# A hybrid attention block on one core: the low part of the queries on 128 rows, queries loaded by halves

## The chip, the cores and the metric

The kernel runs on one core of a Trainium2 chip. A core has the engines TensorE (PE), VectorE (DVE), ScalarE (ACT) and GpSimd (POOL); SyncE (SP) issues the DMAs here, in the order in which they stand on its queue. The metric is the device time of one execution in microseconds, as the median of several runs.

## The reference

One layer over 1024 tokens of width 1024 in float32. After an RMSNorm a combined projection feeds two groups of heads. Group A, which matters here, is sparse attention: an indexer scores all keys for each query, the 256 best are kept, and each of 8 heads (width 64) attends to these.

```
score = sum over index heads of relu(q_idx . k_idx) * w        # masked by chunk
sel   = top 256 keys of each query                             # shared by all heads
logits = q . k / sqrt(64) + bias[bucket(key - query)]          # masked
o_a    = softmax(logits) @ v
```

Group B is gated linear attention. Then come the output projection with a residual, RMSNorm, a SwiGLU feed-forward of width 2816 with a residual, and a last RMSNorm.

## The kernel before

**Two parts for each number.** Matmul operands are float32 values rounded to the matmul's format (fp32r) and a low part that holds the rest. A product then takes three matmuls: high x high, high x low, low x high. In the attention the keys of a head, `Ks[h]`, have both parts in one tile of 128 rows: 64 rows hold the high part and the other 64 the low part (for odd heads the other way round). The high query part, 64 rows, is loaded twice, into both halves of the rows of a tile `q1`, so that one matmul with 128 rows gives high x high plus high x low.

**The low query part** is in a tile `ql`: 128 rows, with two heads one above the other and 4 such head pairs side by side. Its matmul takes only the 64 rows of its head (`r`) and only the high rows of the keys:

```
mm(lg[:, c0:c1], QL[p][r, h // 2, o], Ks[h][r, c0:c1], start=False, stop=True,
```

**One score tile** is made by `softmax(p, h, e)` (L1315): head h and 128 queries, tile t = 2p + e, against the n = 128(t+1) keys up to it. The keys are cut into chunks of up to 512 columns, so tiles 0 to 3 have one chunk and tiles 4 to 7 two. On PE, in this order: for each chunk the high query part times the keys (L1327) and, for the last 256 columns, two matmuls with an identity `eye` that add the position bias `nb` (L1331); then for each chunk the low query part (L1334). DVE adds the mask and takes the row minimum (L1340, for pair 0 L1342), ACT takes the exponential (L1346), DVE a reciprocal (L1348), and POOL scales (L1350). `value` (L1353) transposes the result on PE (L1363), splits it into two parts on ACT (L1375) and DVE (L1378), and multiplies it with the values `Vs` (L1387). `combine` joins the two halves of the output and stores them (`d_ma`, L1419).

**Order.** The program is written by a planner: each piece of work is a generator ("thread") with a rank. It asks for events, for slots of a pool or for time on an engine, and the planner, with its own costs, picks which thread issues its instructions next. The order on every engine and on SP's queue is fixed by this; on the chip semaphores make an instruction wait for its data. Pairs of query tiles come in the order 1, 2, 3, 0. `softmaxes` (L1425) starts score tiles when there are slots (`ahead`: 6 tiles of probabilities, `pl`: 2 wide score banks), and `values` follows. For head 5 of a pair it sets the event "load next", which lets `load_attention` (L1270) load the next pair: the queries (L1296, L1300), then values not yet there (L1307), then the event "load". The event of the last pair lets `main` start `load_out` (rank 1, three pages for each output tile) and the splitting of the output weights (rank 5: ACT L257, POOL L262); `load_attention` has rank 15.

**Pages.** Most tiles of SBUF are pages of one pool of 41. In the attention they hold 8 tiles of keys, up to 8 of values, 4 of bias, up to 5 of masks, 6 of probabilities, 4 of split transposes and 3 of queries for each pair (two `q1`, one `ql`). `finish_pair` gives a pair's pages back when its last output is made.

Of the kernel before, what the change touches and what calls it, by code (L numbers as in the profile page):

```python
# [10 lines left out]
F32R = mybir.dt.float32r  # L11
# [8 lines left out]
P = 128  # L20
# [27 lines left out]
def f32(ap):  # L48
    return ap.bitcast(F32)


PE, ACT, DVE, POOL, DMA = range(5)


def act(n, acc=False):
    return n / 1.2 + (280 if acc else 50)


def dve(n):
    return n / 0.96 + 68  # L60


def pool1(n):
    return n * 0.836 + 160
# [6 lines left out]
def pe(n, passes=1):  # L71
    return n * passes / 2.38
# [249 lines left out]
def block_kernel(ctx: ExitStack, tc: tile.TileContext, a: dict, out: bass.AP, dbg=None):  # L322
    nc = tc.nc
# [16 lines left out]
    def page(shape, dt, name):  # L340
        return big.tile(shape, dt, name=name, tag="pg", bufs=NPG)

    def bank(name="bank"):
        return pp.tile([P, HB], F32, name=name, tag="ps", bufs=4)

    def wide(name="wide"):
        return pp.tile([P, 2 * HB], F32, name=name, tag="pl", bufs=2)

    def small(shape, dt, name, bufs=2):
        return sm.tile(shape, dt, name=name, bufs=bufs)  # L350
# [4 lines left out]
    def quarter(shape, dt, name):  # L355
        return sm.tile(shape, dt, name=name, tag="kb", bufs=NKB)
# [8 lines left out]
    mm = nc.tensor.matmul  # L365
# [97 lines left out]
    fl = Flow()  # L463
    ev = fl.event
    pg = Slots(fl, NPG - NT - 1)
# [4 lines left out]
    LOAD = 2500  # L470
# [376 lines left out]
    d_q = [dr.tile([2, 512, HB], F32, name=f"d_q{i}") for i in range(2)]  # L847
# [398 lines left out]
    Ks, Vs, Q1, QL, nb = {}, {}, {}, {}, []  # L1246
# [23 lines left out]
    def load_attention():  # L1270

        for j in range(NT):
            yield ev("va", j)
        for hf in range(2):
            for c in range(4):
                yield ev("qa", hf, c)
        have = 0
        for at, p in enumerate(PAIRS):
            if at == 0:
                for i in range(4):  # L1280
                    yield ev("nb", i)
                    yield pg
                    yield DMA, 450
                    nb.append(page([P, 2, 2, 256], F32R, "nb"))
                    nc.sync.dma_start(f32(nb[i]), d_nb[i])
            else:
                yield ev("load next", at)
            q = []
            hf, o = p // 2, (p % 2) * 256
            for i in range(2):  # L1290
                yield pg
                yield DMA, 900
                q.append(page([P, 4, 256], F32R, "q1"))
                for s in range(2):
                    src = d_q[hf][0, i * 256:(i + 1) * 256, o:o + 256].rearrange("(h p) n -> p h n", p=64)
                    nc.sync.dma_start(f32(q[i][s * 64:(s + 1) * 64, :, :]), src)  # L1296
            yield pg
            yield DMA, 450
            l = page([P, 4, 256], F32R, "ql")
            nc.sync.dma_start(f32(l), d_q[hf][1, :, o:o + 256].rearrange("(c p) n -> p c n", p=P))  # L1300
            Q1[p], QL[p] = q, l
            ev("Q", p).set(LOAD)
            for j in range(have, 2 * p + 2):
                yield pg
                yield DMA, 450
                Vs[j] = page([P, AH, P], F32R, "V")
                nc.sync.dma_start(f32(Vs[j]), d_va[j])  # L1307
            have = max(have, 2 * p + 2)
            ev("load", p).set(LOAD)

    PB, OP = {}, {}
    units = [(p, h) for p in PAIRS for h in range(AH)]
# [2 lines left out]
    def softmax(p, h, e):  # L1315
        t = 2 * p + e
        n = (t + 1) * P
        o = slice(e * P, (e + 1) * P)
        r = slice((h % 2) * 64, (h % 2) * 64 + 64)
        yield PE, 2 * pe(n) + 2 * pe(256) if t else 380  # L1320
        if t == 4:
            lg, chunks = wide("lg")[:, P:P + n], ((0, 384), (384, 640))
        else:
            lg, chunks = wide("lg") if p else bank("lg"), [(c, min(n, c + HB)) for c in range(0, n, HB)]
        for c0, c1 in chunks:
            d0 = max(c0, n - 256)
            mm(lg[:, c0:c1], Q1[p][h // 4][:, h % 4, o], Ks[h][:, c0:c1], start=True, stop=False,  # L1327
               skip_group_check=True)
            for s in range(2):
                if d0 < c1:  # L1330
                    mm(lg[:, d0:c1], eye, nb[h // 2][:, s, h % 2, 256 - n + d0:256 - n + c1],  # L1331
                       start=False, stop=False, skip_group_check=True)
        for c0, c1 in chunks:
            mm(lg[:, c0:c1], QL[p][r, h // 2, o], Ks[h][r, c0:c1], start=False, stop=True,  # L1334
               skip_group_check=True)
        pb = PB[t, h] = page([P, n], F32, "pb") if p else quarter([P, 256], F32, "pb")[:, :n]
        mn = small([P, 1], F32, "mn", 6)
        yield DVE, dve(n)
        if p:
            nc.vector.tensor_tensor_reduce(pb, lg[:, :n], acc[t][:, :n], 1.0, 3e38, ALU.add, ALU.min, mn)  # L1340
        else:
            nc.vector.tensor_scalar(pb, lg[:, :n], 0.0, 3e38, op0=ALU.add, op1=ALU.min, accum_out=mn)  # L1342
        (pl if p else ps).give()
        yield ACT, act(n, True)
        se = small([P, 1], F32, "sume", 6)
        nc.scalar.activation(pb, pb, AF.Exp, bias=mn, scale=-1.0, accum_out=se)  # L1346
        yield DVE, 75
        nc.vector.reciprocal(se, se)  # L1348
        yield POOL, pool1(n) + 80
        nc.gpsimd.tensor_scalar(pb, pb, se, 1.0, op0=ALU.mult, op1=ALU.mult)  # L1350
        ev("p", t, h).set()
# [73 lines left out]
    def softmaxes():  # L1425
        for _ in range(NAHEAD + NPAIRS):
            yield pg
        at = 0
        for n, (p, h) in enumerate(units):
            if h == 0:  # L1430
                at += 1
                yield ev("load", p)
                if p == 0:
                    ev("softmax").set()
                    fl.spawn(give_back(ahead, NAHEAD), 0)
            for hf in range(p // 2 + 1):
                yield ev("ka", hf, h // 2)
            for e in range(2):
                if p:
                    yield ev("mask", 2 * p + e)  # L1440
                    yield ahead
                    yield pl
                else:
                    yield kb
                    yield ps
                if h == 5 and e == 0:
                    ev("load next", at).set()
                fl.spawn(softmax(p, h, e), 16.5 + n)

    def give_back(slots, n):  # L1450
        for _ in range(n):
            yield slots
            pg.give()

    def values():
        for n, (p, h) in enumerate(units):
            for e in range(2):
                yield ev("p", 2 * p + e, h)
            if h % 2 == 0:
                yield ps  # L1460
                OP[p, h // 2] = bank("av")
            for i in range(p + 1):
                if p:
                    yield pairs
                else:
                    yield hp
                    yield hp
                yield ps
                fl.spawn(value(n, i), 18.2 + n - 0.1 * i)
            if h % 2:  # L1470
                fl.spawn(combine(n), 16 + n)
            if h == 7:
                fl.spawn(finish_pair(p, n), 19 + n)
            if n == 8 * 3 - 1:
                fl.spawn(give_back(pairs, NPAIRS), 0)

    def finish_pair(p, n):
        yield ev("av", n, p)
        pg.give(n=[3 + 8 + 2 + 4, 3 + 1, 3 + 2, 3 + 2 + 6][p])
        ev("pair", p).set()  # L1480


# [717 lines left out]
    def main():  # L2200
# [19 lines left out]
        yield from proj_f(evac_qa, 1)  # L2220
        yield from proj_f(evac_ka, 0)
        fl.spawn(load_attention(), 15)
        fl.spawn(softmaxes(), 16)
        fl.spawn(values(), 17.5)
        yield from proj_f(evac_ka, 1, True)
# [61 lines left out]
```

## Time and profile before

| | us |
|---|---|
| median of 3 runs | 1335.14 (1332.27 to 1335.7) |
| the profiled execution | 1333.15 |
| its span, first to last instruction | 1331.3 |
| PE, DVE, ACT, POOL busy in the span | 1268.2, 968.9, 621.1, 444.1 |

The attention scores run from 417 to 578 us of the span; the first 417 us hold the projections, the indexer with its selection and the linear attention, and from 600 us on come the feed-forward products. Times of rows are microseconds from the span's start. [...]

### The profile page before, as it was taken

The numbers are of one execution on the slowest core, as the hardware profiler recorded it, in microseconds if no ns is written. First come the engines' busy times: TensorE is split into PE (matmuls) and PEld (weight loads), VectorE is DVE, ScalarE is ACT, GpSimd is POOL, SyncE is SP. The second block draws the span as 40 slices with busy tenths as digits, with TensorE's granted clock in tenths as the row PEclk, the third lists the DMA queues.
The fourth block names the chain that finished last, engine by engine and source line by source line (L and its number), as shares of the span: only waits on it lengthen the run. The fifth ranks groups of instructions, "written<-read, shape, count | busy, mean of one in ns | idle before, by whom it ended". The sixth has DMA issues, their size and how long they took to land.

```text
span 1331.3 us, 18081 instructions
## 1 busy us (share of the span) xinstructions
PE 1268.2 (95%) x6074; PEld 1028.8 (77%) x6074; DVE 968.9 (73%) x1900; ACT 621.1 (47%) x1139; POOL 444.1 (33%) x410
## 2 busy tenths in 40 slices
PE   5999999969999999989987999999999999999997
PEld 5878868746787888868865888888888888888886
DVE  5379998989996788724387788889776664435885
ACT  4467678554544677632143444444444432222232
POOL 4324324533311444561244343435333220000351
PEclk8999989979998999989988999999999999999999
DMA  7654221234471233565212676777667549555664
GB/s 217 182 145 127 67 60 49 95 127 167 170 233 46 74 112 112 164 209 206 87 40 80 221 263 235 269 263 266 221 222 237 182 170 381 200 197 190 206 252 174
DMA packets 122812, 230.22 MB, mean 173 GB/s; under 512 B 14120, under 2 KB 70240, under 8 KB 122720
## 3 DMA queue, kind: packets, MB, share of 16 engines
q1 hardware_dynamic: 122720, 229.07, 51.3%
q8 instruction: 48, 0.79, 0.3%
q14 instruction: 44, 0.36, 0.1%
HBM read 146.19 MB, written 82.85 MB: 172 GB/s over the span
## 4 chain that ended last, share of the span: by engine, by line
PE 75%; DVE 16%; issue 3%; DMA 2%; ACT 2%; POOL 1%; SPq 1%; POOLq 0%; DVEq 0%; ACTq 0%
DVE junk_v L756 6%; PE av L1387 3%; PE fc L1769 3%; PE fa L1769 3%; PE fa L1770 3%; PE fc L1770 3%; PE fa L1771 3%; PE fc L1771 3%; PE fb L1771 3%; PE fb L1770 3%; PE da L2085 3%; PE da L2083 3%; PE da L2084 3%; PE fb L1769 3%; PE ptr L1363 3%
## 5 line engine op out<-in xcount | busy, mean ns | idle before, releaser
L1594 POOL TENSOR_TENSOR w<-raw,w 128x512 fp32r<-128x512 f32 x66 | 96.8, 1469 | 181.9 <-ACT w L1730 140.7
L262 POOL TENSOR_TENSOR w<-st,w 128x512 fp32r<-128x512 f32 x68 | 91.3, 1350 | 88.3 <-ACT w L257 87.2
L1730 ACT ACTIVATE w<-raw 128x512 fp32r<-128x512 f32 x132 | 81.7, 626 | 63.0 <-DMA d_wd<-wd 17.1
L756 DVE TENSOR_SCALAR_CACHE_REDUCE junk_v<-acc,thr 128x640 bf16<-128x640 f32 (+3 forms) x128 | 103.6, 809 | 1.9
L762 ACT ACTIVATE junk_a<-acc,thr 128x1024 bf16<-128x1024 f32 x64 | 73.4, 1147 | 44.0 <-DVE thr L788 31.1
L2031 DVE TENSOR_TENSOR da<-U,da 128x512 fp32r<-128x512 f32 x54 | 43.9, 812 | 53.3 <-ACT da L2029 52.9
L1350 POOL TENSOR_SCALAR pb<-pb,sume 128x384 f32<-128x384 f32 (+3 forms) x64 | 47.6, 750 | 99.7 <-DVE sume L1348 79.9
L368 PE MATMUL pj<-w,hT 128*128 128x512 f32 x192 | 78.8, 410 | 1.4 <-DVE spillq L876 1.4
L2029 ACT ACTIVATE da<-U 128x512 fp32r<-128x512 f32 x54 | 33.6, 629 | 95.9 <-PE da L2085 28.2
L1769 PE MATMUL fb<-hc,w 128*128 128x512 f32 x176 | 70.4, 400 | 8.2 <-ACT w L1730 4.2
L368 PE MATMUL pf<-hT,w 128*128 128x512 f32 x192 | 76.7, 400 | 0.0
L1771 PE MATMUL fb<-hc,w 128*128 128x512 f32 x176 | 70.3, 400 | 5.7 <-DVE w L1597 5.7
L369 PE MATMUL pj<-w,hT 128*128 128x512 f32 x192 | 75.7, 394 | 0.0
L370 PE MATMUL pj<-w,hT 128*128 128x512 f32 x192 | 75.6, 394 | 0.0
L370 PE MATMUL pf<-hT,w 128*128 128x512 f32 x192 | 75.5, 393 | 0.0
L369 PE MATMUL pf<-hT,w 128*128 128x512 f32 x192 | 75.5, 393 | 0.0
L1770 PE MATMUL fb<-hc,w 128*128 128x512 f32 x176 | 70.7, 402 | 1.9 <-DVE hc L1597 1.2
L1594 POOL TENSOR_TENSOR wd<-wd 128x512 fp32r<-128x512 f32 x33 | 50.2, 1525 | 65.6 <-ACT wd L1960 60.1
L1960 ACT ACTIVATE wd<-wd 128x512 fp32r<-128x512 f32 x77 | 48.1, 628 | 49.9 <-DMA d_wd<-wd 22.3
L1769 PE MATMUL fc<-hc,w 128*128 128x512 f32 x176 | 68.7, 390 | 0.3 <-DVE gt L1818 0.3
L1769 PE MATMUL fa<-hc,w 128*128 128x512 f32 x176 | 68.7, 390 | 0.0
L2085 PE MATMUL da<-db,da 128*128 128x512 f32 x176 | 68.6, 390 | 0.0
(303 smaller groups left out, 3733.5 us busy)
## 6 DMA issues: line engine op xcount, KB each, us to landing
d_wd<-wd SPq DMA_DIRECT2D x77, 512.0 KB, 3.5
db<-d_wd SPq DMA_DIRECT2D x77, 512.0 KB, 3.4
st<-w_in SPq DMA_DIRECT2D x52, 256.0 KB, 2.8
raw<-w_ffn_gate SPq DMA_DIRECT2D x22, 512.0 KB, 5.2
raw<-w_ffn_up SPq DMA_DIRECT2D x22, 512.0 KB, 4.5
wd<-w_ffn_down SPq DMA_DIRECT2D x44, 256.0 KB, 4.9
d_ux<-gt SPq DMA_DIRECT2D x9, 512.0 KB, 2.6
d_uy<-gt SPq DMA_DIRECT2D x9, 512.0 KB, 2.8
```

The source lines that it names most:

```text
L262: self.nc.gpsimd.tensor_tensor(w[:, 1, :], st, f32(w[:, 0, :]), op=ALU.subtract)
L368: mm(ps, lh, rh, start=first, stop=False)
L369: mm(ps, lh, rl, start=False, stop=False)
L370: mm(ps, ll, rh, start=False, stop=last)
L756: v.tensor_scalar(junk_v[:, :w], acc[ts[i]], col, 0.0, op0=op, op1=ALU.add, accum_out=cnt[:, i:i + 1])
L762: nc.scalar.activation(junk_a[:, :NA[t]], acc[t], AF.Sign, bias=col[:, nv:], scale=-1.0, accum_out=cnt[:, nv:])
L1594: nc.gpsimd.tensor_tensor(dst, src, high, op=ALU.subtract)
L1730: nc.scalar.activation(w4[:, 0], src, AF.Copy)
L1769: mm(b, w[:, 0, kk], h[:, 0, :], start=first, stop=False, skip_group_check=True)
L1770: mm(b, w[:, 0, kk], h[:, 1, :], start=False, stop=False, skip_group_check=True)
L1771: mm(b, w[:, 1, kk], h[:, 0, :], start=False, stop=k == 3, skip_group_check=True)
L2085: mm(bs[t], l[:, 1, tt], r[:, 0, :], start=False, stop=last, skip_group_check=True)
```

## The change

The low part of the queries is now loaded like the high one: 64 rows of a head in both halves of a 128-row tile, so a pair has two `ql` pages instead of one. Its matmul uses all 128 rows and multiplies with both parts of the keys. The queries of a pair are loaded by halves of four heads (`load_queries`): the first half before the values and the event "load", the second after it. `free_queries` gives the two pages of a half back when the eight score tiles of its four heads are done, and `finish_pair` gives back three pages less.

```diff
--- before.py
+++ after.py
@@ -1285,21 +1285,7 @@
                     nc.sync.dma_start(f32(nb[i]), d_nb[i])
             else:
                 yield ev("load next", at)
-            q = []
-            hf, o = p // 2, (p % 2) * 256
-            for i in range(2):
-                yield pg
-                yield DMA, 900
-                q.append(page([P, 4, 256], F32R, "q1"))
-                for s in range(2):
-                    src = d_q[hf][0, i * 256:(i + 1) * 256, o:o + 256].rearrange("(h p) n -> p h n", p=64)
-                    nc.sync.dma_start(f32(q[i][s * 64:(s + 1) * 64, :, :]), src)
-            yield pg
-            yield DMA, 450
-            l = page([P, 4, 256], F32R, "ql")
-            nc.sync.dma_start(f32(l), d_q[hf][1, :, o:o + 256].rearrange("(c p) n -> p c n", p=P))
-            Q1[p], QL[p] = q, l
-            ev("Q", p).set(LOAD)
+            yield from load_queries(p, 0)
             for j in range(have, 2 * p + 2):
                 yield pg
                 yield DMA, 450
@@ -1307,6 +1293,27 @@
                 nc.sync.dma_start(f32(Vs[j]), d_va[j])
             have = max(have, 2 * p + 2)
             ev("load", p).set(LOAD)
+            yield from load_queries(p, 1)
+
+    def load_queries(p, i):
+
+
+        hf, o = p // 2, (p % 2) * 256
+        for part, to in enumerate((Q1, QL)):
+            yield pg
+            yield DMA, 900
+            q = to[p, i] = page([P, 4, 256], F32R, "ql" if part else "q1")
+            for s in range(2):
+                src = d_q[hf][part, i * 256:(i + 1) * 256, o:o + 256].rearrange("(h p) n -> p h n", p=64)
+                nc.sync.dma_start(f32(q[s * 64:(s + 1) * 64, :, :]), src)
+        ev("Q", p, i).set(LOAD)
+
+    def free_queries(p, i):
+        for h in range(4 * i, 4 * i + 4):
+            for e in range(2):
+                yield ev("p", 2 * p + e, h)
+        pg.give(n=2)
+
 
     PB, OP = {}, {}
     units = [(p, h) for p in PAIRS for h in range(AH)]
@@ -1316,7 +1323,6 @@
         t = 2 * p + e
         n = (t + 1) * P
         o = slice(e * P, (e + 1) * P)
-        r = slice((h % 2) * 64, (h % 2) * 64 + 64)
         yield PE, 2 * pe(n) + 2 * pe(256) if t else 380
         if t == 4:
             lg, chunks = wide("lg")[:, P:P + n], ((0, 384), (384, 640))
@@ -1324,14 +1330,14 @@
             lg, chunks = wide("lg") if p else bank("lg"), [(c, min(n, c + HB)) for c in range(0, n, HB)]
         for c0, c1 in chunks:
             d0 = max(c0, n - 256)
-            mm(lg[:, c0:c1], Q1[p][h // 4][:, h % 4, o], Ks[h][:, c0:c1], start=True, stop=False,
+            mm(lg[:, c0:c1], Q1[p, h // 4][:, h % 4, o], Ks[h][:, c0:c1], start=True, stop=False,
                skip_group_check=True)
             for s in range(2):
                 if d0 < c1:
                     mm(lg[:, d0:c1], eye, nb[h // 2][:, s, h % 2, 256 - n + d0:256 - n + c1],
                        start=False, stop=False, skip_group_check=True)
         for c0, c1 in chunks:
-            mm(lg[:, c0:c1], QL[p][r, h // 2, o], Ks[h][r, c0:c1], start=False, stop=True,
+            mm(lg[:, c0:c1], QL[p, h // 4][:, h % 4, o], Ks[h][:, c0:c1], start=False, stop=True,
                skip_group_check=True)
         pb = PB[t, h] = page([P, n], F32, "pb") if p else quarter([P, 256], F32, "pb")[:, :n]
         mn = small([P, 1], F32, "mn", 6)
@@ -1433,6 +1439,9 @@
                 if p == 0:
                     ev("softmax").set()
                     fl.spawn(give_back(ahead, NAHEAD), 0)
+            if h % 4 == 0:
+                yield ev("Q", p, h // 4)
+                fl.spawn(free_queries(p, h // 4), 0)
             for hf in range(p // 2 + 1):
                 yield ev("ka", hf, h // 2)
             for e in range(2):
@@ -1476,7 +1485,7 @@
 
     def finish_pair(p, n):
         yield ev("av", n, p)
-        pg.give(n=[3 + 8 + 2 + 4, 3 + 1, 3 + 2, 3 + 2 + 6][p])
+        pg.give(n=[8 + 2 + 4, 1, 2, 2 + 6][p])
         ev("pair", p).set()
 
 
```

## Rows read from the trace of the kernel before

**Rows 1.** Page, part 1: busy time, share of the span, instructions.
```profile
PE 1268.2 (95%) x6074; PEld 1028.8 (77%) x6074; DVE 968.9 (73%) x1900; ACT 621.1 (47%) x1139; POOL 444.1 (33%) x410
```
**Rows 2.** Windows by stage: per engine busy us (x instructions); then granted clock, DMA share.
```profile
core 0: us, PE busy (x) PEld busy (x) DVE busy (x) ACT busy (x) POOL busy (x), PEclk, DMA share, GB/s
421.00:434.50 13.50, 12.05 (x35) 8.66 (x36) 6.90 (x25) 5.33 (x15) 3.78 (x6) 0.50 0.23 64
434.50:541.30 106.80, 106.80 (x694) 88.12 (x692) 86.45 (x230) 74.95 (x176) 47.38 (x62) 1.00 0.31 95
...
554.60:577.80 23.20, 22.95 (x124) 18.61 (x122) 13.64 (x45) 13.90 (x42) 19.85 (x24) 1.00 0.58 193
577.80:600.00 22.20, 18.41 (x67) 13.01 (x67) 5.59 (x13) 7.94 (x17) 13.36 (x14) 0.85 0.59 196
```
**Rows 3.** Timeline of PE, last projection matmuls and first score tiles.
```profile
416.57 0.39 PE L369 MATMUL pf<-hT,w 128*128 128x512 f32 x1
416.80 0.39 PE L370 MATMUL pf<-hT,w 128*128 128x512 f32 x1
417.02 0.33 PE L1327 MATMUL lg<-K,q 128*128 128x384 f32 x1
417.19 0.39 PE L1331 MATMUL lg<-nb,eye 128*128 128x256 f32 x2
417.51 0.44 PE L1334 MATMUL lg<-K,ql 64*128 64x384 f32 x1
417.89 0.49 PE L1327 MATMUL lg<-K,q 128*128 128x512 f32 x1
418.22 0.40 PE L1331 MATMUL lg<-nb,eye 128*128 128x256 f32 x2
```
**Rows 4.** Timeline of PE, score tiles with two chunks.
```profile
532.67 0.40 PE L1331 MATMUL lg<-nb,eye 128*128 128x256 f32 x2
533.00 0.67 PE L1334 MATMUL lg<-K,ql 64*128 64x512 f32 x2
533.59 0.72 PE L1327 MATMUL lg<-K,q 128*128 128x512 f32 x2
534.15 0.40 PE L1331 MATMUL lg<-nb,eye 128*128 128x256 f32 x2
```
**Rows 5.** Timeline of PE at the lower granted clock.
```profile
422.45 0.79 PE L1327 MATMUL lg<-K,q 128*128 128x512 f32 x1 [2.44 <-DVE mn L1340]
423.05 0.63 PE L1331 MATMUL lg<-nb,eye 128*128 128x256 f32 x2
423.60 0.79 PE L1334 MATMUL lg<-K,ql 64*128 64x512 f32 x1
424.33 0.69 PE L1327 MATMUL lg<-K,q 128*128 128x384 f32 x1
424.81 0.63 PE L1331 MATMUL lg<-nb,eye 128*128 128x256 f32 x2
```
**Rows 6.** Windows of line L1334 alone (the low-part matmuls).
```profile
421.00:434.50 13.50, 3.75 (x5) 1.43 (x5) 0.50 0.23 64
434.50:541.30 106.80, 26.31 (x78) 11.97 (x78) 1.00 0.31 95
...
554.60:577.80 23.20, 3.47 (x10) 1.83 (x10) 1.00 0.58 193
```
**Rows 7.** Windows in the selection stage.
```profile
240.00:260.00 20.00, 18.57 (x86) 15.02 (x85) 19.55 (x48) 7.24 (x14) 9.60 (x7) 1.00 0.44 143
```
**Rows 8.** DMA issues of the queries: KB each, median us to landing.
```profile
q<-d_q SPq DMA_DIRECT2D x16, 256.0 KB, 4.2
ql<-d_q SPq DMA_DIRECT2D x4, 512.0 KB, 6.5
```
**Rows 9.** Timeline: pair 0's last query load, its first score, its head 4.
```profile
514.59 0.55 SPq L1300 DMA_DIRECT2D ql<-d_q  x1
...
535.14 0.33 PE L1327 MATMUL lg<-K,q 128*128 128x128 f32 x1
...
559.87 0.22 PE L1327 MATMUL lg<-K,q 128*128 128x128 f32 x1
```
**Rows 10.** Waits of SP's queue, 380 to 600 us: us in total, times, longest.
```profile
SPq L1307 <- PE pf L370: 18.1, 4, 11.2
SPq L1296 <- PE ptr L1363: 16.9, 3, 11.0
```

## The prediction

> **What bounds the kernel now.** I read the page first: TensorE (PE) is busy for 95% of the span [rows 1], but this is an average. The change touches one stage, the attention, so I cut the span there into stretches by what PE does [rows 2]. From 434.5 to 541.3 us PE is busy for all 106.8 us, VectorE (DVE) for 86.45, ScalarE for 74.95, GpSimd for 47.38. PE sets the pace there and DVE is second at 81%. [...] From 554.6 to 577.8 PE has 22.95 of 23.2 us, but GpSimd has 19.85, since it makes the low parts of the output weights that PE multiplies with. From 577.8 to 600 no engine is near full: a chain of short waits.
>
> A busy PE isn't PE at its peak, so next I read when matmuls start. [rows 3] is the PE timeline around the first scores. While all instructions use 128 rows, starts follow the columns: the 512-column projection matmul takes 416.57 to 416.80, 0.23 us, and the 384-column score 417.02 to 417.19, 0.17. That is 0.057 us per 128 columns, so 0.115 for 256, and the weight loads in between cost nothing visible. Around the 64-row matmul of the low query part (ql) this breaks:
> - the two 256-column identity matmuls before it take 417.19 to 417.51, 0.32 instead of 0.23: 0.09 late;
> - ql, 384 columns, takes 417.51 to 417.89, 0.38 instead of 0.17: 0.21 late;
> - the 512-column score behind it takes 417.89 to 418.22, 0.33 instead of 0.23: 0.10 late.
>
> Together 0.40 us per score tile beyond what its columns take. With two chunks [rows 4] it is the same: identity pair 532.67 to 533.00 (0.10 late), two ql chunks of 512 and 384 columns 533.00 to 533.59 (0.59 instead of 0.40, 0.19 late), two score chunks of 512 behind them 533.59 to 534.15 (0.56 instead of 0.46, 0.10 late). So the price hangs on the two switches, into 64 rows and out again, and not on the number of chunks: each switch costs about 0.1 us before the first matmul of the new shape and 0.1 us more inside its interval. At the half clock [rows 5], where 128 columns take 0.107 us (512 columns in 0.43), the identity pair 423.05 to 423.60 is 0.12 late, ql 423.60 to 424.33 is 0.30 late, the 384-column score 424.33 to 424.81 is 0.16 late: 0.58.
>
> **The change, part by part.**
>
> *ql with 128 rows.* The matmul keeps its columns and count; only its rows become 128. By [rows 3] a matmul among matmuls of its own shape costs its columns, so I take the lateness as gone. As estimates from the 0.40 I take 0.38 us for tiles of pairs 1 to 3, since what stands behind ql isn't always a wide score, and 0.34 for pair 0, whose matmuls have only 128 or 256 columns. The opposite bound is below.
>
> How many, where: 8 heads x 8 query tiles are 64 score tiles; those of tiles 4 to 7 have two chunks. ql's 78 matmuls between 434.5 and 541.3 [rows 6] are 8 tiles of pair 1 (one chunk), 32 of pairs 2 and 3 (64 chunks) and 6 of pair 0. PE's saving: 40 x 0.38 + 6 x 0.34 = 17.2 us, leaving 89.6 us of PE work. But DVE's 86.45 us stay, which is now 96% of that. Two engines that feed each other (DVE empties the score bank and makes the low part of each transposed tile, PE needs both) can't both run without gaps on a fixed order. Where DVE was the busiest engine on mostly independent work it reached 19.55 of 20 us, 98% [rows 7]; now it has 81%. I take 92%, nearer the upper end because with a faster PE its inputs come earlier: 86.45 / 0.92 = 94.0 us, a gain of 12.8. Bounds: 17.2 when PE stays dense, and 5 when DVE only gets to 85% (101.7 us).
>
> *The stretch at half clock.* 5 ql matmuls [rows 6] x 0.58 = 2.9 us of PE time; DVE isn't near its limit. If the clock comes back at the same moment, 2.9 us of half-speed time hold 1.5 us of full-speed work. I take 2; bounds 1.5 and 2.9, and 6 if the denser work brings the clock back earlier (work that took 6.8 us at half speed would take 3.4). The three score tiles before it give nothing: PE then waits 2.44 us for DVE, which is still busy with the keys [rows 5]. What PE saves ahead of that only lengthens the wait.
>
> *Pair 0 beside the output projection.* 10 ql matmuls [rows 6] x 0.34 = 3.4 us of PE. GpSimd's 19.85 us of 23.2 [rows 2] leave room for 3.35 at most, and its order is fixed; I take 1, bounds 0 and 3.4. From 577.8 to 600 nothing is saved; the chain only starts earlier. Behind 600 us PE has the feed-forward products, which follow in order, so I carry the gain to the end in full.
>
> *The loads.* Per pair, four DMAs of 256 KB and one of 512 KB become eight of 256 KB: 12 more issues in all and 2 MB more (q x16 and ql x4 now, landing in 4.2 and 6.5 us [rows 8]). They lie on SyncE's queue well ahead of their use (pair 0's last is issued at 514.59, its first score starts at 535.14 [rows 9]), beside a DMA share of 0.31 [rows 2]; cost 0 under that cover. The first half with its values is on its way before the second is asked for, so nothing is needed earlier than now. Uncovered, four issues and a landing are about 3.2 + 4.2 us, once for each pair: the upper bound 4 x 7.4 = 30 us, the lower 0; I take 0, and follow the one place where it is tight as a rival.
>
> *Pages.* A pair now holds 4 pages of the 41 instead of 3, but gives 2 back after four heads. By the counts in the code, pair 3 with pair 0's queries has just room for both and for the first output tile. An order shifted by this I count at nothing, with 2 us either way.
>
> Sum: 12.8 + 2 + 1 = 15.8. The profiled execution took 1333.15 us (span 1331.3): 1317.4. The median of the runs is 2.0 above it, so I place the forecast between, at **1318**.
>
> [...] Row first: the 512-column matmuls of [rows 3] start 0.23 us apart with a full-row weight load for each, so such a load lies under the matmul before it. [...]
>
> **The rivals.**
> 1. *PE stays dense.* DVE keeps up, and the clock may return early. For it: DVE idles for 20 of the 106.8 us today, so it has work done ahead. Against: 86.45 of 89.6. Gain 17.2 + 2.9 + 3.4 = 23.5, with the clock 27: 1306 to 1310.
> 2. *Half of the lateness stays.* Only the 0.1 us before the first matmul of a new shape goes, and ql's own load stays exposed: 0.2 per tile. 46 x 0.2 = 9.2, + 1 + 0.5 = 10.7: 1322. For it: nothing in the trace shows a full-row ql. Against: [rows 3], full-row loads hidden everywhere else.
> 3. *DVE becomes the bound.* It reaches 85%: gain 5 + 1.5 + 0 = 6.5: 1327. It decides when GpSimd's and ScalarE's steps between the engines (now behind PE) come last.
> 4. *The lateness isn't the row switch*, but something that stays, such as the write into the same bank: gain 0, 1333 to 1335. Against: it appears again on the way out, where ql is followed by another bank [rows 3].
> 5. *Slower: pair 0's second half comes late.* Its two pages are now asked for after the event that lets the output tiles and output weights take pages, and these rank ahead of it. Today the last of pair 0's queries is issued at 514.59; head 4 starts at 559.87 [rows 9]. The second half must be issued by about 552 (3.2 + 4.2 us before). If it got pages only when pair 3 ends, near 554, it would cost 2 to 3 us. To be slower overall it must be issued over 16 us past that, near 570, and heads 4 to 7 wait for it. SyncE's queue does wait for pages for up to 11.2 us at once today [rows 10], so it can happen; but 18 us beyond the point is more than any wait shown.
>
> **How the numbers follow.** Forecast (gain 10 to 20): 0.58. Rival 1: 0.16. Rival 2: 0.08 (its time lies in the forecast's own span). Rival 3: 0.09. Rival 4: 0.05. Rival 5 as a net loss: 0.04. The likeliest case itself spans 1313 to 1323. Rivals 1 and 3 are half taken in by a range of 1308 to 1328, which leaves out about 0.2. A measurement here tells 0.3%, 4 us, from no change: faster 0.90, same 0.06, slower 0.04.
>
> **What would show it.** In the new trace the low-part matmuls read 128*128 with 128 rows; an identity pair of 256 columns takes 0.23 us up to ql's start and ql itself 0.057 us per 128 columns, at both ends. The stretch from the clock's return to the first scores of pair 0's head 3 lasts about 94 us instead of 107, DVE is busy for over 90% of it, and PE shows gaps that end on DVE (rival 3 if DVE is under 87%, rival 1 if PE has none). Intervals of 0.1 us that remain at ql mean rival 2 or 4. The wrong step would most likely be the 92%; next, a loss behind 541 us through pages, seen as a late second half of pair 0's queries.

## The result, and the profile after

The changed kernel takes 1319.97 us (median of 4 runs, 1315.0 to 1325.23); the kernel before, on the same chip, 1335.42. The ratio is 0.9876, 95% interval 0.9842 to 0.9909. The profiled execution took 1317.16 us, its span 1315.3, 16.0 less than before.

First the timeline of PE around the first score tiles, which answers to [rows 3]:

```profile
416.66 0.39 PE L370 MATMUL pf<-hT,w 128*128 128x512 f32 x1
416.89 0.33 PE L1333 MATMUL lg<-K,q 128*128 128x384 f32 x1
417.06 0.39 PE L1337 MATMUL lg<-nb,eye 128*128 128x256 f32 x2
417.29 0.34 PE L1340 MATMUL lg<-K,ql 128*128 128x384 f32 x1
417.47 0.39 PE L1333 MATMUL lg<-K,q 128*128 128x512 f32 x1
417.70 0.40 PE L1337 MATMUL lg<-nb,eye 128*128 128x256 f32 x2
```

In these rows "x2" is two instructions of one kind merged. The 512-column score is shown 0.39 us long, yet the next matmul starts 0.23 us after it, so I read costs between starts. The low-part matmul now reads 128*128. The identity pair takes 417.06 to 417.29, 0.23 us; ql, 384 columns, 417.29 to 417.47, 0.18; the 512-column score behind it 0.23. Nothing is late. Two chunks, answering to [rows 4]:

```profile
515.78 0.40 PE L1337 MATMUL lg<-nb,eye 128*128 128x256 f32 x2
516.02 0.58 PE L1340 MATMUL lg<-K,ql 128*128 128x512 f32 x2
516.44 0.63 PE L1333 MATMUL lg<-K,q 128*128 128x512 f32 x2
516.90 0.40 PE L1337 MATMUL lg<-nb,eye 128*128 128x256 f32 x2
```

The pair takes 0.24, the two ql chunks 0.42 (0.59 before), the two score chunks behind them 0.46 (0.56 before). And at the lower granted clock, answering to [rows 5]:

```profile
422.63 0.63 PE L1337 MATMUL lg<-nb,eye 128*128 128x256 f32 x2
423.06 0.63 PE L1340 MATMUL lg<-K,ql 128*128 128x512 f32 x1
423.49 0.52 PE L1333 MATMUL lg<-K,q 128*128 128x384 f32 x1
423.81 0.63 PE L1337 MATMUL lg<-nb,eye 128*128 128x256 f32 x2
```

0.43, 0.43 and 0.32 us: exactly the columns at 0.107 us per 128. Then the windows, answering to [rows 2] (columns as there):

```profile
421.00:427.70 6.70, 5.66 (x20) 5.06 (x21) 3.95 (x17) 3.53 (x11) 2.43 (x4) 0.50 0.00 0
427.70:431.20 3.50, 3.50 (x28) 3.38 (x28) 3.22 (x12) 3.01 (x9) 1.37 (x3) 0.99 0.59 148
431.20:522.80 91.60, 90.93 (x685) 85.81 (x685) 84.32 (x228) 73.07 (x172) 48.52 (x63) 1.00 0.49 131
536.60:580.40 43.80, 36.52 (x178) 29.00 (x177) 20.42 (x59) 19.88 (x56) 31.30 (x37) 0.92 0.53 173
```

The half clock ends at 427.7 us instead of 434.5. Behind it PE is busy for 90.93 of 91.6 us and DVE for 84.32, 92%.

To compare runs I use marks that don't depend on where an execution starts. **Stretch A** goes from DVE's reading of pair 1's ninth score tile to its reading of pair 0's sixth (435.9 to 541.5 us before, 431.2 to 522.8 after). **Stretch B** goes from ScalarE's copy of pair 3's last output to DVE's addition for the first output tile (554.1 to 597.8 before, 536.6 to 580.4 after). The 16.0 us of the two spans are: ahead of A, from the first score tile read, 17.8 to 13.5, 4.3 gained (and 0.4 ahead of that); A, 105.6 to 91.6, 14.0 gained; between A and B, 12.6 to 13.8, 1.2 lost; B, 43.7 to 43.8; behind B, 733.5 to 734.9, 1.4 lost.

All runs, with A and B from each one's profile, and how long the clock stayed at its lower level behind the first scores. The profile of before_on_dve is of an execution of 4351 us, far outside its ten other times (1333.4 to 1344.2), so only its ratio is used:

| run | ratio to before (95%) | A, us | B, us | half clock, us |
|---|---|---|---|---|
| before | | 105.6 | 43.7 | 13.7 |
| changed | 0.9876 (0.9842 to 0.9909) | 91.6 | 43.8 | 6.8 |
| after_again | 0.9878 (0.9829 to 0.9928) | 91.6 | 45.5 | 6.8 |
| rows64 | 1.0014 (0.9990 to 1.0038) | 105.4 | 46.2 | 10.2 |
| whole_loads | 0.9886 (0.9841 to 0.9931) | 97.7 | 39.7 | 3.4 |
| per_chunk64 | 1.0102 (1.0063 to 1.0141) | 118.0 | 43.8 | 10.2 |
| per_chunk128 | 0.9903 (0.9861 to 0.9944) | 91.5 | 43.6 | 6.8 |
| no_ql | one time, 1314.09 us | 88.6 | 42.4 | 6.8 |
| last_whole | 0.9865 (0.9814 to 0.9917) | 91.3 | 42.4 | 0 |
| weights_on_dve | 0.9801 (0.9760 to 0.9842) | 91.5 | 36.6 | 6.8 |
| before_on_dve | 1.0016 (0.9993 to 1.0040) | – | – | – |
| both_on_dve | 0.9854 (0.9821 to 0.9888) | 91.6 | 41.6 | 6.8 |

### The profile page after: what moved, and what is told of

The parts are those of the page before. It is cut to its first block, busy times and chain, and to the rows that moved or that the text cites. A ratio compares the mean times of both kernels' runs of the same rounds, so it can differ in the third digit from the quotient of the medians.

```text
span 1315.3 us, 18107 instructions
## 1 busy us (share of the span) xinstructions
PE 1244.9 (95%) x6074; PEld 1024.0 (78%) x6074; DVE 971.1 (74%) x1900; ACT 619.6 (47%) x1139; POOL 444.5 (34%) x410
## 4 chain that ended last, share of the span: by engine, by line
PE 70%; DVE 18%; DMA 4%; issue 3%; ACT 2%; POOL 1%; SPq 1%; POOLq 0%; DVEq 0%; ACTq 0%
DVE junk_v L756 6%; PE da L2094 3%; PE da L2093 3%; PE da L2092 3%; PE fa L1780 3%; PE fa L1778 3%; PE fa L1779 3%; PE fc L1778 3%; PE av L1393 3%; PE fc L1780 3%; PE fc L1779 3%; PE fb L1780 3%; PE fb L1779 2%; PE fb L1778 2%; PE db L2093 2%
## 5 line engine op out<-in xcount | busy, mean ns | idle before, releaser
L1739 ACT ACTIVATE w<-raw 128x512 fp32r<-128x512 f32 x132 | 81.6, 626 | 63.2 <-DMA d_wd<-wd 15.9
L762 ACT ACTIVATE junk_a<-acc,thr 128x1024 bf16<-128x1024 f32 x64 | 73.4, 1147 | 44.1 <-DVE thr L788 31.2
```

The costliest lines, as they stand in the source:

```text
L762: nc.scalar.activation(junk_a[:, :NA[t]], acc[t], AF.Sign, bias=col[:, nv:], scale=-1.0, accum_out=cnt[:, nv:])
L1739: nc.scalar.activation(w4[:, 0], src, AF.Copy)
```

## The experiments

The theory: what the gain consists of is the two switches between 64-row and 128-row matmuls in each score tile. The rivals: the loads by halves and the order that they bring; or a lateness that goes with the chunk and not with the switch.

**after_again**, the changed kernel beside the others, no edit.

> The changed kernel once more, beside the others. Both theories: about 16 us under the kernel before (ratio near 0.988). If the granted clock comes back at 427.7 us in this profile too, the stretch of half clock behind 421 us is 6.8 us long as in the first profile; if it comes back at 434.5 us, the time should be some 2 to 3 us higher for it.

Ratio 0.9878, A again 91.6. The clock came back after 6.8 us here too, yet the profiled execution was 8.3 us longer than the first: its first score tile was read 5.4 us later, behind a longer stretch at half clock that lies ahead of the scores (last section). So A and B tell more than a single time.

**rows64**: the changed kernel with the old rows.

```diff
+        r = slice((h % 2) * 64, (h % 2) * 64 + 64)
...
-            mm(lg[:, c0:c1], QL[p, h // 4][:, h % 4, o], Ks[h][:, c0:c1], ...
+            mm(lg[:, c0:c1], QL[p, h // 4][r, h % 4, o], Ks[h][r, c0:c1], ...
```

> The changed kernel, same pages, loads and order of instructions, but the low-part matmul takes the 64 rows of the high key part again. Theory (row switches): all of the gain goes, ratio to the kernel before near 1.00 (0.997 to 1.004), the intervals from the identity pair to ql and from ql on are late by 0.1 and 0.2 us again, and PE's busy stretch from 431 to 523 us is about 14 us longer. Rival (the loads by halves and the order they bring do it): ratio stays near 0.988.

The whole gain goes: 1.0014, A 105.4 against 105.6 before. PE's timeline in that run, at the same place:

```profile
416.69 0.39 PE L1338 MATMUL lg<-nb,eye 128*128 128x256 f32 x2
417.01 0.44 PE L1341 MATMUL lg<-K,ql 64*128 64x384 f32 x1
417.39 0.50 PE L1334 MATMUL lg<-K,q 128*128 128x512 f32 x1
417.72 0.40 PE L1338 MATMUL lg<-nb,eye 128*128 128x256 f32 x2
```

Identity pair 0.32, ql 0.38, the score behind it 0.33: the lateness of [rows 3] to the hundredth, with the order, pages and loads of the changed kernel. So the rows are the cause, and loads, pages and order bring nothing by themselves that can be measured.

**whole_loads**: the kernel before with the 128-row low part alone, four pages for each pair from its load to its end.

```diff
-            l = page([P, 4, 256], F32R, "ql")
-            nc.sync.dma_start(f32(l), d_q[hf][1, :, o:o + 256].rearrange("(c p) n -> p c n", p=P))
+            for i in range(2):
+                ...
+                    nc.sync.dma_start(f32(l[i][s * 64:(s + 1) * 64, :, :]), src)
...
-            mm(lg[:, c0:c1], QL[p][r, h // 2, o], Ks[h][r, c0:c1], start=False, stop=True,
+            mm(lg[:, c0:c1], QL[p][h // 4][:, h % 4, o], Ks[h][:, c0:c1], start=False, stop=True,
...
-        pg.give(n=[3 + 8 + 2 + 4, 3 + 1, 3 + 2, 3 + 2 + 6][p])
+        pg.give(n=[4 + 8 + 2 + 4, 4 + 1, 4 + 2, 4 + 2 + 6][p])
```

> The kernel before with the 128-row low part alone: four query pages for each pair, loaded together and given back at the pair's end. Theory (row switches): most of the gain, but pages run short where two pairs' queries lie side by side, so the next pair's loads come late: ratio 0.988 to 0.996, with PE waiting at the start of pair 3 or of pair 0. Rival (halves matter by themselves): ratio near 1.00.

The shortage came where it was expected. SyncE's queue before pair 3:

```profile
467.56 2.85 SPq L1304 DMA_DIRECT2D ql<-d_q  x4
470.71 0.35 SPq L1311 DMA_DIRECT2D V<-d_va  x1
473.59 18.14 SPq L1422 DMA_DIRECT2D d_ma<-mxa  x3
491.82 0.56 SPq L1311 DMA_DIRECT2D V<-d_va  x1
```

One block of values is issued at 470.71, the other only at 491.82, behind the stores of pair 2. From pair 2's first score tile to pair 3's first took 44.1 us instead of the changed kernel's 34.8. But the planner's order fills that time with transposes and values that would come later: PE's waits in A are 3.1 us in all, for DVE and ScalarE and none for a load. The next pair then takes 38.6 instead of 41.4 and B is 39.7 instead of 43.8. From the first score tile read to the last output tile it took 232.3 us, the changed kernel 235.9 and 237.9, but with 6.8 us at half clock in it against 13.7 in each of those. The ratio, 0.9886, is the same within the intervals: the halves and the early freeing buy nothing that can be measured.

**per_chunk64**: the kernel before with ql behind each chunk, so that a tile with two chunks switches four times.

```diff
                        start=False, stop=False, skip_group_check=True)
-        for c0, c1 in chunks:
             mm(lg[:, c0:c1], QL[p][r, h // 2, o], Ks[h][r, c0:c1], start=False, stop=True,
```

> The kernel before with the 64-row low-part matmul directly behind each chunk instead of behind all chunks: the 32 score tiles with two chunks switch rows four times instead of twice. Theory (each pair of switches costs about 0.35 us of PE): 32 x 0.35 = 11 us slower, ratio 1.007 to 1.009. Rival (the lateness goes with the chunk, or with the write into the bank, not with the switch): within 2 us of the kernel before.

A grew by 12.4 us, to 118.0, which holds all 32 tiles with two chunks: 0.39 us for each added pair of switches; ratio 1.0102. **per_chunk128** is the same order in the changed kernel.

> The changed kernel with its 128-row low-part matmul directly behind each chunk: the same order as in per_chunk64, without switches of rows. Theory (the switch costs, not the order): as the changed kernel, ratio near 0.988, the stretch from pair 1's ninth score tile to pair 0's sixth within 1 us of 91.6 us. Rival (the order of the chunks cost per_chunk64 its time): ratio 0.995 or more.

A is 91.5, so the order of the chunks costs nothing, and the switches cost all of it. The ratio, 0.9903, is that of the changed kernel within the intervals.

**no_ql**: the changed kernel without the low-part matmul.

```diff
...
-        for c0, c1 in chunks:
-            mm(lg[:, c0:c1], QL[p, h // 4][:, h % 4, o], Ks[h][:, c0:c1], start=False, stop=True,
-               skip_group_check=True)
...
```

> The changed kernel without the low-part matmul; it leaves out low query part x keys, the loads stay. In the stretch of 91.6 us from pair 1's ninth score tile to pair 0's sixth that takes 14.1 us of columns (31360 at 0.23 us per 512) from PE. Theory now (PE set the pace there, DVE still had slack): the stretch falls to 86 to 88 us and DVE is busy for 96 to 98% of it, since its 84 us are then the floor. Rival (the prediction's step: DVE and PE hold each other at about 92%): the stretch stays at 90 us or more.

A fell to 88.6 us, between the two expectations: 3.0 less, although 14.1 us of PE's columns are gone. The windows view of this run over A (columns as in [rows 2]):

```profile
432.70:521.30 88.60, 80.93 (x604) 74.16 (x603) 83.39 (x229) 71.78 (x169) 48.28 (x62) 1.00 0.48 127
```

The shares of its chain of waits over A, by engine and line:

```profile
by line: DVE pt L1381 23.4%; issue 19.4%; DVE pb L1343 13.5%; ACT pb L1349 8.6%; DVE so L1411 6.5%; ACT pt L1378 6.0%; PE ptr L1366 4.4%; PE av L1390 4.4%; POOL pb L1353 3.8%; ACT lo L1405 2.3%; DVE sume L1351 2.2%; PE lg L1333 1.8%; DVE mn
```

DVE is busy for 94% and its lines, with ScalarE's, make up some 62% of the chain; PE, busy for 80.93 us, has gaps. In the changed kernel the chain over A reads:

```profile
by line: PE av L1393 28.6%; PE ptr L1369 24.5%; PE lg L1333 15.7%; PE lg L1340 14.8%; PE lg L1337 10.0%; DVE pb L1346 2.3%; DVE pt L1384 1.5%; ACT pb L1352 1.1%; DVE pb L1348 0.8%; issue 0.5%; DVE sume L1354 0.2%; DVEq L1346 0.0%; DVE mn L1
```

There PE still holds nearly the whole chain, but the chain through DVE and ScalarE lies only 3 us behind it: of a further 14.1 us off PE, 3.0 come through.

**last_whole**: for the last pair both halves are asked for ahead of the event.

```diff
+            if p == PAIRS[-1]:
+                yield from load_queries(p, 1)
             ev("load", p).set(LOAD)
-            yield from load_queries(p, 1)
+            if p != PAIRS[-1]:
+                yield from load_queries(p, 1)
```

> The changed kernel, but for the last pair both halves of the queries are asked for ahead of the event that starts output tiles and output weights. Theory (the second half's pages compete with the output projection and cost what was lost behind pair 0): the stretch from pair 3's last output copy to the first output tile's end, 43.8 us, falls by 1 to 2 us. Rival (the output projection waits for its weights anyway): 43 to 45 us as before, ratio the same as the changed kernel's within its interval.

B is 42.4, 1.4 less, and the stretch between A and B 12.5 instead of 13.8. That fits the theory in size; but in B this execution had 3.4 us at half clock and the first one 6.8, and the ratio can't tell the two kernels apart. Not settled.

**weights_on_dve**: DVE makes every second low part of the output weights (`self.proj` is the number of weight tiles ahead of them).

```diff
...
-                yield POOL, pool2(HB)
-                self.low(st, w)
+                if len(self.items) - todo + n >= self.proj and n % 2:
+                    yield DVE, dvf(HB)
+                    self.nc.vector.tensor_tensor(w[:, 1, :], st, f32(w[:, 0, :]), op=ALU.subtract)
+                else:
+                    yield POOL, pool2(HB)
+                    self.low(st, w)
...
```

> The changed kernel, but every second low part of the output weights is made by DVE instead of GpSimd. Theory (with the scores faster, the output projection beside pair 0 runs at GpSimd's pace, so the rest of the saving is lost there): the stretch from pair 3's last output copy to the first output tile's end falls from 43.8 to 39 to 41 us, ratio 0.984 to 0.986. Rival (a chain through the weight DMAs and ScalarE holds it): 43 us or more, no gain.

B fell by 7.2 us to 36.6, more than expected, and the ratio to 0.9801. This version beats both kernels: each of its four times (1307.3 to 1312.1) lies below all eight of the changed kernel (1315.0 to 1325.5). The windows view of its B:

```profile
536.70:573.30 36.60, 32.68 (x178) 26.33 (x177) 25.00 (x66) 19.56 (x56) 24.68 (x30) 1.00 0.68 208
```

Not all of the 7.2 us was waiting. PE is busy for 32.7 us here and for 36.5 in B of the changed kernel, with 178 matmuls in both: the changed kernel's execution had 6.8 us of B at half clock, this one none. PE's idle time fell by the other 3.4 us. The waits in B of the changed kernel (engine and line, releaser: us in total, times, longest):

```profile
ACT w L257 <- DMA st<-w_out: 11.3, 6, 2.7
...
PEld oa L369 <- POOL w L262: 5.4, 6, 1.8
...
PE oa L369 <- POOL w L262: 3.6, 4, 1.5
```

The same of weights_on_dve:

```profile
ACT w L257 <- DMA st<-w_out: 6.3, 4, 3.0
...
PEld oa L373 <- POOL w L262: 2.6, 2, 1.5
...
PE oa L373 <- POOL w L262: 1.9, 2, 1.1
```

PE's wait for GpSimd falls from 3.6 to 1.9 us, and ScalarE's for the weights' DMA from 11.3 to 6.3; in the code a staging buffer comes free when the low part is made.

**before_on_dve**: the same edit in the kernel before.

> The kernel before, with every second low part of the output weights made by DVE. Theory (GpSimd holds the output projection only once the scores are faster): before, PE had 22.95 of the 23.2 us there and no wait for GpSimd ended late, so only the chain behind it can shrink: the stretch from pair 3's last output copy to the first output tile's end falls from 43.7 by 0 to 4 us, ratio 0.997 to 1.000. Rival (GpSimd held it in the kernel before as well): it falls by 6 to 8 us as with the changed kernel, ratio 0.994 to 0.996.

Ratio 1.0016: no gain. That fits PE's wait for GpSimd in the kernel before, from 541.3 to 600 us:

```profile
PE oa L369 <- POOL w L262: 0.8, 2, 0.6
```

It is 0.8 us against 3.6 in the changed kernel, so this limit is felt only with the change. Whether the faster scores bring it or the new order isn't separated: PE's order from pair 0's sixth tile on differs between the two kernels, and rows64, which has the new order with slow scores, waits 1.9 us. **both_on_dve** is last_whole and weights_on_dve together.

> weights_on_dve and last_whole together. Theory (they act on the same stretch, which already fell to 36.6 us): within 2 us of 36.6, ratio 0.979 to 0.982 as weights_on_dve. Rival (pages and GpSimd are two separate limits): 34 us or less, ratio 0.978 or less.

B is 41.6 and the ratio 0.9854: neither expectation. The edit that gained on the changed kernel gained nothing clear on last_whole (0.9865). PE's order in this stretch came out otherwise in each of these versions, so the gain of weights_on_dve may be the order's as well as GpSimd's; that is not settled.

## Why the prediction was right, step by step

**The lateness goes with the switch of rows: right.** rows64 and per_chunk64 with per_chunk128 show it from both sides, in the size read from [rows 3] (0.40; measured 0.39 for an added pair of switches). Rival 4 is out, and so is rival 2: ql's own interval is 0.18 us with a full-row weight load. Where the second 0.1 us of a switch lies, the weight loads (PEld) around the first score tile differ. Before:

```profile
417.51 0.18 PEld L1334 LDWEIGHTS lg<-K,ql 64*128 64x128 f32 x1
417.88 0.19 PEld L1327 LDWEIGHTS lg<-K,q 128*128 128x128 f32 x1 [0.19 <-issue]
```

and after:

```profile
417.18 0.19 PEld L1340 LDWEIGHTS lg<-K,ql 128*128 128x128 f32 x1
417.30 0.19 PEld L1333 LDWEIGHTS lg<-K,q 128*128 128x128 f32 x1
```

Before, the first load of a new shape starts together with its matmul (417.51 and 417.89 [rows 3]), so it doesn't lie under the matmul ahead; after, the same loads start 0.11 and 0.17 us ahead of their matmuls (417.29 and 417.47). So in these rows a full-row load between full-row matmuls starts under the matmul ahead, and ql's interval of 0.18 us shows none of it. What takes the 0.1 us ahead of the first matmul of the new shape isn't shown.

**0.38 us for each tile: a little too high.** I added up, for all matmuls of A in both traces, the distance to the next start less the columns at 0.057 us per 128 (the 512-column projection matmuls before the scores start 0.227 us apart). At ql's borders this fell by 15.9 us for 46 tiles: 4.2 between the identity pair and ql, 8.5 in ql's intervals, 3.2 in those behind it. That is 0.345 for each tile, 15.9 us against the 17.2 of the sum. The term behind ql was mis-sized: 0.07 on average, not 0.10. A first score chunk is late before its second chunk in both kernels, switch or not: by 0.07 us on average before, by 0.05 after.

**DVE at 92%, the stretch at 94.0 us: right in size, not in what it said.** DVE reached 92%, in 91.6 us, so the gain was 14.0 instead of 12.8. But it didn't hold PE up: of PE's 15.9 us only 2.1 came back as new lateness, and PE was busy for 99%. That the share met the 92% of the step is luck: it is DVE's 84.32 us over the time that PE left, and no limit of DVE's. So the first half of rival 1 came true, on a smaller saving. no_ql shows that the limit which the step spoke of exists, 3 us further on.

**Half clock, 2 us: mis-sized, with the upper bound nearer.** 4.3 us were gained, with the clock back 6.8 us earlier; the step had 6 as its bound for that. It doesn't look like chance alone: with 64 rows the profiles show 13.7, 10.2 and 10.2 us at half clock there, without such matmuls 6.8 or less in all eight (granted clock from 420 to 440 us: 0.66 and 0.74 twice against 0.83 to 1.00). Why the clock came back earlier isn't shown.

**Pair 0 beside the output projection, 1 us: wrong sign.** From pair 0's sixth tile to the end of B it took 56.3 us before and 57.6 after, 1.3 lost. The step saw GpSimd's 19.85 us but counted only on its room, 3.35. In the new trace the output projection waits longer for its weights: PE's wait for GpSimd is 3.6 us instead of 0.8. Part of this can be the new order: rows64 has it too, with slow scores, and took 60.2 us for this stretch, 17.1 of them at half clock, with 1.9 us of that wait. weights_on_dve got 7.2 us in B, of which 3.8 went with the clock; the times of before_on_dve show no gain. Which of the two causes made the loss stays open.

**Loads at 0, and rival 5: right, and close.** The last low part of pair 0's queries is issued late, as that rival described it:

```profile
499.04 2.30 SPq L1308 DMA_DIRECT2D q<-d_q  x2
...
531.09 1.26 SPq L1308 DMA_DIRECT2D ql<-d_q  x2
536.27 2.84 SPq L247 DMA_DIRECT2D st<-w_out  x2
```

Its fellow for the high part goes at 499.04, this one at 531.09; head 4's first score starts at 542.97. The DMA view of this stretch (530 to 541 us) has its landing:

```profile
ql<-d_q SPq DMA_DIRECT2D x2, 256.0 KB, 6.5
```

The second of the two, issued at 531.7, landed at 538.3, so 4.7 us were left. The carry to the end in full was right to 1.4 us, and two profiles of the changed kernel differ by 1.0 there (734.9 and 735.9).

The errors went both ways (+1.2 in A, +2.3 at half clock, -2.3 at pair 0, -1.4 behind B, +0.4 ahead of the scores) and left 16.0 us against a sum of 15.8. The mechanism was right; that the total came so close is luck.

## What to carry to other kernels

Read PE by the distance between starts: a matmul on half the rows cost its columns like a full one here (from ql's first chunk to its second, medians in A: 0.336 us for 512 columns and 0.282 for 384 on 64 rows, 0.233 and 0.177 on 128, so 0.054 and 0.056 for 128 columns more, with 0.10 of the switch on top on 64 rows), and between full ones each pair of switches cost 0.35 to 0.4 us here, more than the widest of these matmuls itself (0.23 us). Filling the rows, even with a product that adds little, took that away (15.9 us of PE in A); putting matmuls of one shape side by side saved part of it (12.4 us between per_chunk64 and the kernel before). When the engine that sets the pace gets faster, look at once at the second and third: here the chain through DVE was 3 us behind, and in the next stage PE's wait for GpSimd grew from 0.8 to 3.6 us.

## What the runs showed of the hardware that I had not expected

A stretch at half clock that lies outside the change makes up much of the difference between profiles. It falls where PE works on the linear attention and projections beside the selection. The granted clock from 240 to 300 us is 0.89 in seven profiles (before, changed, rows64, per_chunk64, last_whole, weights_on_dve, both_on_dve), 0.83 in no_ql, 0.77 in after_again and 0.74 in whole_loads and per_chunk128: between 14 and 31 us of the 60 at half clock. In this order the first score tile is read at 417.0 to 419.8 us, at 420.0, at 423.1, and at 428.7 and 426.0. Of the 8.3 us between the two profiles of the changed kernel, 5.4 lie ahead of that read; per_chunk128's read comes 8.3 us later than in the first of them, half of what the change brought, and the changed matmuls only follow. Kernels that differ by 1% are better compared over the stretch in question than by the time of one execution.
